# Value-pair operands in rows, and three small edits, in a one-layer hybrid decoder

## The chip, the cores and the metric

The kernel runs on one core of one Trainium2 chip, as one launch. The metric is the device time of an execution in microseconds; the time given for a kernel is the median of several runs. The profile of a kernel is one execution taken by the hardware profiler. Its engines are named PE (TensorE, matmuls), PEld (its weight loads), DVE (VectorE), ACT (ScalarE), POOL (GpSimd) and SP (SyncE, which issues the loads); L12 is line 12 of the kernel.

## The reference

One layer of a decoder on x of 512 tokens by 1024 channels, all in fp32:

```python
proj = x @ w_in                       # q, k, v of three mixers, and 3 x 1024 gate columns
o_da = diff_attention(...)            # 4 heads, two softmax maps each
o_sb = stick_breaking_attention(...)  # 8 heads of 64: A = sig(z) * prod of later (1 - sig(z))
o_dl = dilated_attention(...)         # 3 groups (dilation 1, 4, 16) x 4 heads of 128
merged = (g[:, :, 0] * (o_da @ w_branch_da) + g[:, :, 1] * (o_sb @ w_branch_sb)
          + g[:, :, 2] * (o_dl @ w_branch_dil))
x = layer_norm(ALPHA * x + merged @ w_out, ln1_g, ln1_b)
c = square(relu(x @ w_up)) @ w_down
ple = sigmoid(x @ w_ple_gate) * (p @ w_ple)        # p: 512 x 256, the embedding
x = layer_norm(ALPHA * x + c + ple, ln2_g, ln2_b)
```

## The kernel before, in words

Every fp32 operand of a large product is split into a high part rounded to the format fp32r and the rest, and a product is three matmuls: high by high, high by low, low by high. Weights stream from HBM in chunks of 128x1024 through a ring of six raw buffers (the loads are issued by SP); ScalarE casts a chunk to its high part `wh` (L243) and VectorE subtracts to get the low part `wl` (L245), each in a ring of six. x lies transposed in SBUF as `xhT` and `xlT`, eight blocks k of 128 channels by 512 tokens.

The work is a list of items, each a group of matmuls into a PSUM bank and an evacuation. A main loop goes through the items in order; before each item, and in the middle of those whose `mm` yields, it calls `step()`, which advances the attention heads that are active and the generators in `pending`. So heads' small matmuls are laid between the items of the projections. PSUM has two banks of the tag `mm` and six of the tag `at`; SBUF has 48 slots of 128x512 that all other tiles share. A tile gets a slot when its first write is scheduled, and that write waits until a slot is free. The order of each engine's instructions is laid out when the program is built, in program order as far as inputs and buffers allow, with ready instructions going ahead of blocked ones.

The last two groups of dilated values (`dl_v` 1 and 2) are computed together by `value_pair` as seven products of half-size blocks (p = 1, 2, 7, 6, 4, 5, 3 in that order, two items r = 0, 1 of 12 matmuls each, L465 to L467). The stationary operand of a matmul is here a piece of x, 128 channels by 128 tokens, where the tokens are those of one residue modulo 4. For p = 7, 6, 4 and 5 these pieces come from sums of x, made by `value_forms` from tiles `xr` (x loaded again, eight slots) into tiles `fr` and split into `u7`, `u6`, `u4` and `u5` with tokens side by side. For p = 1, 2 and 3 they are read in place, every fourth element of `xhT` and `xlT` (the table `vf`, L364). `value_forms` is put in `pending` four items ahead of the pair, waits `WAIT` = 5 steps, and then makes one form or its split a step.

Dilated head 0 runs at the same time: scores L1805 (dilation 1) and L1821 (the two others), biases and row maxima on VectorE (L1808, L1829), exponentials on ScalarE (L1814, L1836), small products L1846 and L1848 that bring the denominators of the groups together from `r0` (L1839) and `r1` (L1842), and later transposes L1889 and L1898.

A stick-breaking head (`sb_head`) holds its scores in three banks: key block 0 in 512 columns, block 1 in 384, and blocks 2 and 3 side by side in 256 each. After the logarithms, a product with a triangular matrix sums over later keys inside a block (L1666, high and low part), and products with ones (L1670) bring in the blocks behind.

`wout_items` multiplies the merged branches by `w_out`: two halves of 512 columns, four token tiles tt each, 24 matmuls over k = 0 to 7 (L887 to L889). Its stationary operands come from `merged_T[h, th, kp]`, transposes (L794) that ScalarE copies (L798) and VectorE subtracts from (L799): h is the half of k, th the half of the tokens. Those of th = 1 are turned between the first tiles: h = 1 after tile 0, h = 0 after tile 1. Then `ple_items` computes the embedding's product, eight items of six matmuls (L955 to L957) into `at` banks, evacuated by ScalarE (L961), while the first layer norm runs (L848 on ScalarE, L846 to L862 on VectorE) and its transposes (L924) lie between the items.

Of the kernel before, what the change touches and what calls it, by code (L numbers as in the profile page):

```python
# [10 lines left out]
F32 = mybir.dt.float32  # L11
F32R = mybir.dt.float32r  # L12
# [6 lines left out]
P = 128  # L19
# [36 lines left out]
def trunk(tc, a, out):  # L56
    nc = tc.nc
    es = ExitStack()
    with es:
# [14 lines left out]
        def slot(name, dt=F32):  # L74
            return big.tile([P, 512], dt, name=nm(name), tag="s", bufs=NSLOT)
# [190 lines left out]
        def item(cs, mm, ev, need=None, bank=None, size=1.0):  # L266
            items.append({"c": cs, "mm": mm, "ev": ev, "need": need, "bank": bank, "size": size})
# [7 lines left out]
        xhT = one.tile([P, 8, 512], F32R, name="xhT", tag="XH", bufs=1)  # L275
        xlT = one.tile([P, 8, 512], F32R, name="xlT", tag="XL", bufs=1)
        xh = [xhT[:, k, :] for k in range(8)]
        xl = [xlT[:, k, :] for k in range(8)]
# [49 lines left out]
        def first_item():  # L328
# [28 lines left out]
            def ev(ps):  # L357
# [3 lines left out]
        HB = slice(0, 256)  # L361
        HC = slice(256, 512)

        vf = {p: [[(xh[k][:, 2 * th + r::4], xl[k][:, 2 * th + r::4]) for r in range(2)] for k in range(ks, ks + 4)]  # L364
              for p, ks, th in ((1, 0, 0), (2, 4, 0), (3, 4, 1))}
        vsum = [[dram.tile([P, 1024], F32, name=f"vsum{m}_{i}") for i in range(2)] for m in range(2)]
        v_from = [None]

# [19 lines left out]
        def value_forms():  # L388

            xr = [slot("xr") for _ in range(8)]  # L390
            for k, t in enumerate(xr):
                i = nc.gpsimd.dma_start(t, xt[:, k, :])
                tc.add_manual_dep(getattr(i, "ins", i), lows[-1].name, mybir.DependencyInfo(
                    mybir.DependencyClass.Sync, mybir.DependencyReason.DATA), reason="not ahead of time")

            def blk(kh, k, th):
                return xr[4 * kh + k].rearrange("p (t c) -> p c t", c=4)[:, 2 * th:2 * th + 2, :]

            def new():
                ts = [slot("fr") for _ in range(2)]  # L400
                return ts, [ts[k // 2].rearrange("p (k c t) -> p k c t", k=2, c=2)[:, k % 2] for k in range(4)]

            def parts(p, ts):
                form(vf, p, ts)
                vf[p] = [[(h[:, r * P:r * P + P], lo[:, r * P:r * P + P]) for r in range(2)] for h, lo in vf[p]]

            def neg_sub(o, i, j):
                nc.vector.scalar_tensor_tensor(o, i, -1.0, j, op0=OP.mult, op1=OP.subtract)

            for _ in range(WAIT):  # L410
                yield
            f7, o7 = new()
            with tc.issue_after(st["low"]):
                for k in range(4):
                    nc.vector.tensor_sub(o7[k], blk(1, k, 1), blk(0, k, 1))
            parts(7, f7)
            yield
            f6, o6 = new()
            with tc.issue_after(st["low"]):
                for k in range(4):  # L420
                    neg_sub(o6[k], o7[k], blk(0, k, 0))
            yield
            parts(6, f6)
            yield
            f4, o4 = new()
            for k in range(4):
                neg_sub(o4[k], o6[k], blk(1, k, 0))
            yield
            parts(4, f4)
            yield  # L430
            yield
            f1, o1 = new()
            for k in range(4):
                nc.vector.tensor_sub(o1[k], blk(0, k, 0), blk(0, k, 1))
            yield
            parts(5, f1)
            yield

        WAIT = 5

# [436 lines left out]
        def wout_items():  # L877
            for half in range(2):
                cs = [chunk(a["wo"][half, c].rearrange("p k n -> p (k n)"), 1024) for c in range(4)]
                for tt in range(4):  # L880
                    def mm(ps, tt=tt, cs=cs):
                        for k in range(8):
                            c = cs[k // 2]
                            s = slice((k % 2) * 512, (k % 2) * 512 + 512)
                            h, lo = merged_T[k // 4, tt // 2, k % 4 // 2]
                            q = slice(k % 2 * 256 + tt % 2 * P, k % 2 * 256 + tt % 2 * P + P)
                            nc.tensor.matmul(ps, h[:, q], c["h"][:, s], start=k == 0, stop=False)  # L887
                            nc.tensor.matmul(ps, h[:, q], c["l"][:, s], start=False, stop=False)
                            nc.tensor.matmul(ps, lo[:, q], c["h"][:, s], start=False, stop=k == 7)  # L889

                    def ev(ps, tt=tt, half=half):
                        y = xn.pop((tt, half))
                        if not half:
                            x1sum[tt] = small("lsm", 2)
                        i = nc.vector.scalar_tensor_tensor(y, y, ALPHA, ps, op0=OP.mult, op1=OP.add,
                                                           accum_out=x1sum[tt][:, half:half + 1])
                        st["added"] = getattr(i, "ins", i)
                        x1[tt, half] = y
                        if half:
                            pending.append(ln1_gen(tt))  # L900
                    item(cs if tt == 3 else [], mm, ev, need=cs, bank=at_bank)
                    for t in {0: [(1, 1, 0), (1, 1, 1)], 1: [(0, 1, 0), (0, 1, 1)]}.get(tt, ()) if not half else ():
                        turn_item(*t)
# [41 lines left out]
        def ple_items():  # L945
            cs = [chunk(a["wp"][half].rearrange("p k n -> p (k n)"), 1024) for half in range(2)]
            for half in range(2):
                for tt in range(4):
                    def mm(ps, tt=tt, half=half):
                        c = cs[half]  # L950
                        for k in range(2):
                            s = slice(k * 512, k * 512 + 512)
                            q = slice(tt * P, tt * P + P)
                            h, lo = pTs[k]
                            nc.tensor.matmul(ps, h[:, q], c["h"][:, s], start=k == 0, stop=False)  # L955
                            nc.tensor.matmul(ps, h[:, q], c["l"][:, s], start=False, stop=False)
                            nc.tensor.matmul(ps, lo[:, q], c["h"][:, s], start=False, stop=k == 1)  # L957

                    def ev(ps, tt=tt, half=half):
                        t = slot("ple")  # L960
                        nc.scalar.copy(t, ps)  # L961
                        ple[tt, half] = t
                    item([cs[half]] if tt == 3 else [], mm, ev, need=cs, bank=at_bank)


        sums_first = set()
# [490 lines left out]
        tri_r = one.tile([P, P], F32R, name="tri_r")  # L1457
# [151 lines left out]
        def sb_head(hd):  # L1609
# [5 lines left out]
            bank = [at_bank() for _ in range(3)]  # L1615
            for kb, bi, c0, n in reversed(blk):
                m = mask_b.rearrange("p a b -> p (a b)") if kb == 3 else mask_b[:, 1, :]
                nc.tensor.matmul(bank[bi][:, c0:c0 + (n if kb == 3 else P)], identb, m, start=kb != 2, stop=False,
                                 skip_group_check=True)
# [3 lines left out]
            w = [512, 384, 512]  # L1623
            sph, spl, later = {}, {}, {}
            for bi in (2, 1, 0):
                n = w[bi]
                ps = bank[bi][:, :n]
# [9 lines left out]
                h = slot("sph", F32R)[:, :n]  # L1637
                lo = slot("spl", F32R)[:, :n]
# [7 lines left out]
                if bi == 2:  # L1646
# [3 lines left out]
                    hl = slot("smp", F32R)  # L1650
# [3 lines left out]
                elif bi == 1:  # L1654
                    nc.vector.tensor_add(e[:, 128:384], e[:, 128:384], sm)
                    h = slot("smh", F32R)[:, :n]
# [4 lines left out]
                yield  # L1661
            ah, al = {}, {}
            for kb, bi, c0, n in reversed(blk):
                ps = bank[bi][:, c0:c0 + n]
                for hl in (sph, spl):
                    nc.tensor.matmul(ps, tri_r, hl[bi][:, c0:c0 + n], start=False, stop=False, skip_group_check=True)  # L1666
                if kb < 3:
                    n2, hl = later[kb]
                    for t in hl:
                        nc.tensor.matmul(bank[bi][:, c0 + n - n2:c0 + n], ones_r, t, start=False, stop=False,  # L1670
                                         skip_group_check=True)
                if kb == 3:
                    continue
                n = w[bi]
                e = slot("a")[:, :n]
                nc.scalar.activation(e, bank[bi][:, :n], AF.Exp)
                h = slot("ah", F32R)[:, :n]
                lo = slot("al", F32R)[:, :n]
                nc.vector.tensor_copy(h, e)
                nc.vector.tensor_sub(lo, e, h.bitcast(F32))  # L1680
                ah[bi], al[bi] = h, lo
                if kb != 1:
                    yield
# [12 lines left out]
            t = slot("ot")  # L1696
# [461 lines left out]
```

## Time and profile before

| | |
|---|---|
| time, median of 3 runs | 1040.13 us (1039.84 to 1040.6) |
| the profiled execution | 1040.08 us |
| its span, first to last instruction | 1038.1 us |
| granted TensorE clock, mean | 0.998 |
| busy: PE, PEld | 1028.0, 881.2 us |
| busy: DVE, ACT, POOL | 787.0, 591.7, 180.1 us |
| moved by DMA | 249.21 MB |

The busy time of PE is a union of overlapping, modelled spans, so that it covers short waits too; how fast TensorE goes is read from the distance between the starts of its matmuls. The stages are found by time: the stick-breaking heads up to 226 us, the value pair from 235 to 278 us, w_out from 607 to 658 us, the embedding from 658 to 672 us. The timeline's columns are start and duration in us, engine, line, operation, tiles, shapes and count; a bracket gives the idle time of the engine before the instruction and who ended it.

### The profile page before, as it was taken

To read this page: it belongs to the slowest core of one execution; us is meant where nothing else is said; L and a number is where in the kernel's file an instruction comes from. 1 tells how busy PE (TensorE), PEld (TensorE's weight loads), DVE (VectorE), ACT (ScalarE), POOL (GpSimd) and SP (SyncE) were. 2 spreads that over 40 slices of the span, in tenths; PEclk is the share of its full clock that TensorE was granted. 3 is DMA by queue.
4 is the path that set the end of the run, shared out by engine and by line. 5 is a ranking of instruction groups with operands and counts; after the bars stand their busy time and mean duration, and the time that the engine had idled before them with its cause. 6 is when DMAs were issued, how large, how long until landed. Compare 5 with 4: busy or idle time off the path is not lost.

```text
span 1038.1 us, 15050 instructions
## 1 busy us (share of the span) xinstructions
PE 1028.0 (99%) x5448; PEld 881.2 (85%) x5448; DVE 787.0 (76%) x1412; ACT 591.7 (57%) x1010; POOL 180.1 (17%) x271
## 2 busy tenths in 40 slices
PE   9999999999999999999999999999999999999997
PEld 6888888889888888888888888889999889889886
DVE  6888667769765657779688885798768877877965
ACT  7566544536434645676675743775666556555651
POOL 0002411120211232411011040111111111111001
PEclk9999999999999999999999999999999999999999
DMA  8449968485976999977789795579999999998612
GB/s 309 121 156 271 277 193 217 120 290 144 285 182 222 271 272 294 238 205 199 227 269 235 267 320 182 160 222 319 331 290 315 301 306 340 303 295 279 235 57 81
DMA packets 71322, 249.21 MB, mean 240 GB/s; under 512 B 8808, under 2 KB 9592, under 8 KB 71248
## 3 DMA queue, kind: packets, MB, share of 16 engines
q0 software_dynamic: 32464, 116.21, 44.8%
q1 hardware_dynamic: 38208, 131.13, 35.1%
q8 instruction: 43, 0.70, 0.3%
q10 hardware_dynamic: 576, 0.92, 0.2%
q14 instruction: 31, 0.25, 0.1%
HBM read 246.10 MB, written 98.59 MB: 332 GB/s over the span
## 4 chain that ended last, share of the span: by engine, by line
PE 94%; DVE 2%; ACT 1%; DMA 1%; issue 1%; SPq 0%; POOL 0%; DVEq 0%; ACTq 0%; POOLq 0%
PE mm L87 10%; PE mm L88 10%; PE mm L89 10%; PE at L1261 4%; PE at L1262 4%; PE at L1263 4%; PE at L599 3%; PE at L600 3%; PE at L601 3%; PE mm L496 2%; PE mm L498 2%; PE mm L497 2%; PE at L89 1%; PE at L88 1%; PE at L87 1%; PE at L761 1%
## 5 line engine op out<-in xcount | busy, mean ns | idle before, releaser
L243 ACT CAST wh<-raw 128x1024 fp32r<-128x1024 f32 x257 | 268.6, 1049 | 242.0 <-PE mm L88 134.2
L245 DVE TENSOR_TENSOR wl<-raw,wh 128x1024 fp32r<-128x1024 f32 x257 | 312.7, 1223 | 112.9 <-ACT wh L243 111.3
L87 PE MATMUL mm<-xhT,wh 128*128 128x512 f32 x302 | 119.1, 394 | 0.0
L89 PE MATMUL mm<-xhT,wl 128*128 128x512 f32 x302 | 118.2, 391 | 0.0
L88 PE MATMUL mm<-xlT,wh 128*128 128x512 f32 x302 | 118.1, 391 | 0.0
L1261 PE MATMUL at<-wh,hh 128*128 128x512 f32 x188 | 73.7, 392 | 0.0
L87 PE MATMUL mm<-x1hT,wh 128*128 128x256 f32 x256 | 73.7, 288 | 0.0
L1262 PE MATMUL at<-wl,hh 128*128 128x512 f32 x188 | 73.7, 392 | 0.0
L1263 PE MATMUL at<-wh,hl 128*128 128x512 f32 x188 | 73.1, 389 | 0.0
L88 PE MATMUL mm<-x1lT,wh 128*128 128x256 f32 x256 | 72.2, 283 | 0.0
L89 PE MATMUL mm<-x1hT,wl 128*128 128x256 f32 x256 | 71.8, 283 | 0.0
L89 PEld LDWEIGHTS mm<-xhT,wl 128*128 128x128 f32 x302 | 56.8, 188 | 11.9
L87 PEld LDWEIGHTS mm<-xhT,wh 128*128 128x128 f32 x302 | 56.7, 188 | 11.0
L88 PEld LDWEIGHTS mm<-xlT,wh 128*128 128x128 f32 x302 | 56.7, 188 | 10.8
L87 PEld LDWEIGHTS mm<-x1hT,wh 128*128 128x128 f32 x256 | 48.7, 190 | 4.8 <-ACT up L1195 3.0
L88 PEld LDWEIGHTS mm<-x1lT,wh 128*128 128x128 f32 x256 | 48.8, 191 | 1.5
L89 PEld LDWEIGHTS mm<-x1hT,wl 128*128 128x128 f32 x256 | 48.6, 191 | 0.0
L1095 POOL DMA_DIRECT2D usum<-in_wu_dram x32 | 28.3, 921 | 101.6 <-DMA usum<-usum 34.8
L1095 POOL DMA_DIRECT2D dsum<-in_wd_dram x28 | 25.6, 936 | 102.5 <-DMA dsum<-dsum 37.0
L1263 PEld LDWEIGHTS at<-wh,hl 128*128 128x128 f32 x188 | 35.3, 188 | 7.7
L1261 PEld LDWEIGHTS at<-wh,hh 128*128 128x128 f32 x188 | 35.5, 189 | 6.0
L1262 PEld LDWEIGHTS at<-wl,hh 128*128 128x128 f32 x188 | 35.5, 189 | 5.5
(601 smaller groups left out, 2677.2 us busy)
## 6 DMA issues: line engine op xcount, KB each, us to landing
usum<-in_wu_dram POOLq DMA_DIRECT2D x48, 512.0 KB, 9.0
dsum<-in_wd_dram POOLq DMA_DIRECT2D x42, 512.0 KB, 8.9
raw<-in_wt_dram SPq DMA_DIRECT2D x38, 512.0 KB, 5.1
raw<-usum SPq DMA_DIRECT2D x32, 512.0 KB, 7.7
raw<-dsum SPq DMA_DIRECT2D x28, 512.0 KB, 7.0
raw<-in_wd_dram SPq DMA_DIRECT2D x25, 512.0 KB, 6.1
raw<-in_wu_dram SPq DMA_DIRECT2D x24, 512.0 KB, 7.6
raw<-in_wv_dram SPq DMA_DIRECT2D x18, 512.0 KB, 5.7
```

What stands on the lines that cost most here:

```text
L87: nc.tensor.matmul(ps, wh, xh, start=start, stop=False, skip_group_check=True)
L88: nc.tensor.matmul(ps, wh, xl, start=False, stop=False, skip_group_check=True)
L89: nc.tensor.matmul(ps, wl, xh, start=False, stop=stop, skip_group_check=True)
L243: i = nc.scalar.copy(h, raw)
L245: i = nc.vector.tensor_sub(lo, raw, h.bitcast(F32))
L599: nc.tensor.matmul(ps, h[:, q], c["h"][:, n], start=go, stop=False, skip_group_check=True)
L600: nc.tensor.matmul(ps, h[:, q], c["l"][:, n], start=False, stop=False, skip_group_check=True)
L601: nc.tensor.matmul(ps, lo[:, q], c["h"][:, n], start=False, stop=end, skip_group_check=True)
L1095: i = nc.gpsimd.dma_start(o, i, accum_op=OP.add, max_dma_last_dim=4096)
L1261: nc.tensor.matmul(ps, h[:, q], c["h"][:, s], start=go, stop=False, skip_group_check=True)
L1262: nc.tensor.matmul(ps, h[:, q], c["l"][:, s], start=False, stop=False, skip_group_check=True)
L1263: nc.tensor.matmul(ps, lo[:, q], c["h"][:, s], start=False, stop=end, skip_group_check=True)
```

## The change

Four edits. `in_rows` copies the strided pieces of x for p = 1, 2 and 3 by ScalarE into tiles `vh` and `vl` where a piece's 128 tokens lie side by side: eight copies of 128x256 into four slots for each p, in two steps of four. Those of p = 1 are made in the last two of the five steps that `value_forms` waits; those of p = 2 begin in the step that splits form 6, so that forms 4 and its split come one step later; those of p = 3 begin in the step that splits form 5. In the third tile of the first half of w_out the order of k is 4 to 7, then 0 to 3. The embedding's items of odd tt in the first half take a bank of the tag `mm`. In a stick-breaking head the triangular products of key blocks 2 and 3 become one of 512 columns for each of the two parts.

```diff
--- before.py
+++ after.py
@@ -361,8 +361,24 @@
         HB = slice(0, 256)
         HC = slice(256, 512)
 
-        vf = {p: [[(xh[k][:, 2 * th + r::4], xl[k][:, 2 * th + r::4]) for r in range(2)] for k in range(ks, ks + 4)]
-              for p, ks, th in ((1, 0, 0), (2, 4, 0), (3, 4, 1))}
+        vf = {}
+
+        def in_rows(p, ks, th):
+
+            vf[p] = []
+            for kp in range(2):
+                ts = []
+                for x, name in ((xhT, "vh"), (xlT, "vl")):
+                    t = slot(name, F32R)
+                    i = x[:, ks + 2 * kp:ks + 2 * kp + 2, :].rearrange("p k (t c) -> p k c t", c=4)
+                    o = t.rearrange("p (k c t) -> p k c t", k=2, c=2)
+                    for k in range(2):
+                        nc.scalar.copy(o[:, k], i[:, k, 2 * th:2 * th + 2].bitcast(F32))
+                    ts.append(t)
+                vf[p] += [[tuple(t[:, 256 * k + r * P:256 * k + r * P + P] for t in ts) for r in range(2)]
+                          for k in range(2)]
+                yield
+
         vsum = [[dram.tile([P, 1024], F32, name=f"vsum{m}_{i}") for i in range(2)] for m in range(2)]
         v_from = [None]
 
@@ -407,8 +423,9 @@
             def neg_sub(o, i, j):
                 nc.vector.scalar_tensor_tensor(o, i, -1.0, j, op0=OP.mult, op1=OP.subtract)
 
-            for _ in range(WAIT):
+            for _ in range(WAIT - 2):
                 yield
+            yield from in_rows(1, 0, 0)
             f7, o7 = new()
             with tc.issue_after(st["low"]):
                 for k in range(4):
@@ -421,20 +438,19 @@
                     neg_sub(o6[k], o7[k], blk(0, k, 0))
             yield
             parts(6, f6)
-            yield
+            yield from in_rows(2, 4, 0)
             f4, o4 = new()
             for k in range(4):
                 neg_sub(o4[k], o6[k], blk(1, k, 0))
             yield
             parts(4, f4)
             yield
-            yield
             f1, o1 = new()
             for k in range(4):
                 nc.vector.tensor_sub(o1[k], blk(0, k, 0), blk(0, k, 1))
             yield
             parts(5, f1)
-            yield
+            yield from in_rows(3, 4, 1)
 
         WAIT = 5
 
@@ -878,15 +894,17 @@
             for half in range(2):
                 cs = [chunk(a["wo"][half, c].rearrange("p k n -> p (k n)"), 1024) for c in range(4)]
                 for tt in range(4):
-                    def mm(ps, tt=tt, cs=cs):
-                        for k in range(8):
+                    ks = (4, 5, 6, 7, 0, 1, 2, 3) if tt == 2 and not half else range(8)
+
+                    def mm(ps, tt=tt, cs=cs, ks=ks):
+                        for k in ks:
                             c = cs[k // 2]
                             s = slice((k % 2) * 512, (k % 2) * 512 + 512)
                             h, lo = merged_T[k // 4, tt // 2, k % 4 // 2]
                             q = slice(k % 2 * 256 + tt % 2 * P, k % 2 * 256 + tt % 2 * P + P)
-                            nc.tensor.matmul(ps, h[:, q], c["h"][:, s], start=k == 0, stop=False)
+                            nc.tensor.matmul(ps, h[:, q], c["h"][:, s], start=k == ks[0], stop=False)
                             nc.tensor.matmul(ps, h[:, q], c["l"][:, s], start=False, stop=False)
-                            nc.tensor.matmul(ps, lo[:, q], c["h"][:, s], start=False, stop=k == 7)
+                            nc.tensor.matmul(ps, lo[:, q], c["h"][:, s], start=False, stop=k == ks[-1])
 
                     def ev(ps, tt=tt, half=half):
                         y = xn.pop((tt, half))
@@ -960,7 +978,8 @@
                         t = slot("ple")
                         nc.scalar.copy(t, ps)
                         ple[tt, half] = t
-                    item([cs[half]] if tt == 3 else [], mm, ev, need=cs, bank=at_bank)
+                    item([cs[half]] if tt == 3 else [], mm, ev, need=cs,
+                         bank=None if tt % 2 and not half else at_bank)
 
 
         sums_first = set()
@@ -1661,9 +1680,9 @@
                 yield
             ah, al = {}, {}
             for kb, bi, c0, n in reversed(blk):
-                ps = bank[bi][:, c0:c0 + n]
-                for hl in (sph, spl):
-                    nc.tensor.matmul(ps, tri_r, hl[bi][:, c0:c0 + n], start=False, stop=False, skip_group_check=True)
+                for hl in (sph, spl) if kb != 2 else ():
+                    nc.tensor.matmul(bank[bi][:, :w[bi]], tri_r, hl[bi], start=False, stop=False,
+                                     skip_group_check=True)
                 if kb < 3:
                     n2, hl = later[kb]
                     for t in hl:
```

## The prediction

> **What bounds the kernel now.** I read the page first: span, busy shares and the chain that ended last.
>
> ```profile
> span 1038.1 us, 15050 instructions
> ...
> PE 1028.0 (99%) x5448; PEld 881.2 (85%) x5448; DVE 787.0 (76%) x1412; ACT 591.7 (57%) x1010; POOL 180.1 (17%) x271
> ...
> PE 94%; DVE 2%; ACT 1%; DMA 1%; issue 1%; SPq 0%; POOL 0%; DVEq 0%; ACTq 0%; POOLq 0%
> ```
>
> TensorE is busy for 99% of the span and carries 94% of the chain. A change therefore pays only where it shortens TensorE's own stream or closes a hole in it, and it costs wherever TensorE comes to wait. The profiled execution took 1040.08 us: 1038.1 of span and 1.98 around it. It lies 0.05 below the median of the runs, 1040.13, so one sum serves for both. A measurement of this kernel can tell about 0.2% from no change, that is 2.08 us: faster means below 1038.05 and slower above 1042.21.
>
> Then I read the weight loads of the value pair by line (columns: shortest, median and longest ns, first and last start) and the timeline of TensorE and its loads (start us, duration us).
>
> ```profile
> L465 PEld LDWEIGHTS at<-wh,xhT x16: 308/310/311, 239.7 to 277.6; 128*128 128x128 f32 x16
> ...
> L465 PEld LDWEIGHTS mm<-wh,u6h x4: 188/188/188, 254.6 to 256.7; 128*128 128x128 f32 x4
> ...
> 272.67 0.31 PEld L465 LDWEIGHTS at<-wh,xhT 128*128 128x128 f32 x1
> ...
> 278.31 1.71 PEld L1910 LDWEIGHTS at<-pt,dl_v 128*128 128x128 f32 x8
> ...
> 254.65 0.19 PEld L465 LDWEIGHTS mm<-wh,u6h 128*128 128x128 f32 x1
> ...
> 260.08 0.19 PEld L465 LDWEIGHTS mm<-wh,u4h 128*128 128x128 f32 x1
> ...
> 239.71 0.60 PE L465 MATMUL at<-wh,xhT 128*128 128x512 f32 x1
> 240.15 0.40 PE L466 MATMUL at<-wl,xhT 128*128 128x512 f32 x1
> ...
> 263.71 0.47 PE L465 MATMUL at<-wh,u4h 128*128 128x512 f32 x1
> 264.03 0.39 PE L466 MATMUL at<-wl,u4h 128*128 128x512 f32 x1
> ...
> 243.45 0.30 PEld L1846 LDWEIGHTS at<-r,fold 128*128 128x128 f32 x2 [0.40 <-DVE r L1839]
> ```
>
> A load with every fourth element of x takes 310 ns, one from a row 188.
>
> **Rows for products 1, 2 and 3.** Product 3 is 24 matmuls between 272.67 and 278.31: 5.64 us. Product 6, from rows, takes 260.08 - 254.65 = 5.43 us. The difference is 0.21, and three products have strided operands: 0.63 us less. The load thus stays mostly hidden, as it is prefetched under the matmul before it. It shows where the matmuls before are short: after the small matmuls of dilated head 0 the second strided matmul starts 0.44 us after the first (239.71 to 240.15), in rows 0.32 (263.71 to 264.03). Such blocks (L1805, L1821, L1846, L1848) stand four times ahead of a strided matmul: 4 x 0.12 = 0.48 us less.
>
> The Trainium skill, TensorE: Matmul & The Clock Gate, LDWEIGHTS (loading the stationary operand), makes the load a matter of its column count alone; by it rows would gain nothing here. The trace disagrees, 310 against 188 ns with the same 128 columns. The skill's SBUF - State Buffer, on the 16-byte lines under Door 1: The DMA port swizzle, charges each access that crosses into a new line, which four fp32 elements of step do; the two durations agree with that one, and it would charge the new copies as well.
>
> What the rows add is 24 ScalarE copies of 128x256.
>
> ```profile
> L1195 ACT COPY up<-mm 128x256 f32<-128x256 f32 x16 | 5.8, 363 | 0.0
> ...
> L271 ACT CAST u6h<-fr x2: 620/621/622, 232.1 to 233.2; 128x512 fp32r<-128x512 f32 x2
> ...
> L408 DVE SCALAR_TENSOR_TENSOR fr<-fr,xr x8: 610/620/640, 230.9 to 240.7; 128x256 f32<-128x256 f32 x8
> ...
> L1201 DVE TENSOR_TENSOR hid<-mm,up x16: 417/425/425, 714.8 to 957.7; 128x256 f32<-128x256 f32 x16
> ...
> 220.00:225.00 5.00, 5.00 (x25) 4.06 (x24) 3.67 (x6) 1.06 (x1) 0.99 (x2) 1.00 1.05 374
> 225.00:230.00 5.00, 5.00 (x25) 4.20 (x24) 3.33 (x6) 2.89 (x5) 0.00 (x0) 1.00 0.86 278
> 230.00:235.00 5.00, 5.00 (x26) 4.22 (x24) 4.86 (x8) 2.57 (x4) 0.52 (x1) 1.00 0.55 206
> 235.00:240.00 5.00, 5.00 (x31) 4.96 (x30) 3.61 (x13) 2.16 (x9) 0.00 (x0) 1.00 0.32 113
> ```
>
> No row shows ScalarE reading SBUF at this step. From below it costs the contiguous copy of the same size, 0.36 us; from above a contiguous one of twice the size, 0.62. VectorE pays 620 instead of 425 ns for 256 elements where it reads x at this step, 0.2 more, so I take 0.5, between them: 12 us for 24, 4 for each product (2.9 to 5.0). ScalarE (the fourth busy figure of the windows) does 1.06 + 2.89 + 2.57 + 2.16 = 8.7 us in 220 to 240, so 11.3 are free. The eight copies of product 1, due at 235, and the eight of product 2, due at about 242, need 8 (5.8 to 9.9). They fit, and cost TensorE nothing, if they get their buffers in time. Without that cover product 2 starts late by what is left of its 4 us. Those of product 3 are made at the items of product 7, ahead of product 6 and so 18 us (254.65 to 272.67) before their use.
>
> Buffers are the tight point.
>
> ```profile
> 239.10 2.24 DVE L408 SCALAR_TENSOR_TENSOR fr<-fr,xr 128x256 f32<-128x256 f32 x4 [1.35 <-PE at L1821]
> ...
> 237.84 0.40 ACT L1814 ACTIVATE L<-L,nm 128x128 f32<-128x128 f32 x1 [3.06 <-DVE nm L1812]
> ...
> 239.78 0.59 ACT L472 COPY dl_v<-mm 128x512 f32<-128x512 f32 x1
> ...
> 243.21 0.18 DVE L1839 TENSOR_TENSOR r<-st,exf 128x32 f32<-128x32 f32 x1
> ...
> 214.51 1.05 ACT L243 CAST wh<-raw 128x1024 fp32r<-128x1024 f32 x1 [5.11 <-PE mm L88]
> ```
>
> L408 reads nothing that L1821 writes; it waits because its new tile takes a slot that L1821's operands hold. Counting the code's live tiles at 238 us I get all 48 slots: 4 outputs of heads, 4 bias tables, 4 value tiles, 16 q and k tiles, 8 of xr, 2 fr, 8 of u7 and u6, 2 of L0. The change wants up to 8 more there. Two things give way without harm: u6, cast by 234 and first read at 254.65, and form 4 (L408), which the change puts one step later. The copies wait for nothing but a slot, so the build may also set them earlier: ScalarE idles 5.11 us ahead of 214.51, and the same count of tiles leaves 8 slots free at 213. I take no stall from slots in the forecast and keep it as a rival.
>
> The later form 4 also moves 2.24 us of VectorE work from ahead of L1829 and L1839, for which TensorE's L1846 idles 0.40. With the copies near L1814, whose sums L1839 reads, I count half of it, 0.20 (from 0.40 gained to some microseconds lost, below).
>
> **Third w_out tile.** It now begins with k 4 to 7, whose transposes were turned after the first tile, and reads those just turned 2.7 us (12 matmuls of 0.226) later.
>
> ```profile
> 623.19 1.03 PE L794 MATMUL mm<-ident,b 128*128 128x128 f32 x8
> ...
> 624.47 0.50 PE L887 MATMUL at<-wh,mh 128*128 128x512 f32 x1 [0.24 <-ACT mh L798]
> ...
> 659.55 1.03 PE L924 MATMUL at<-ident,xn 128*128 128x128 f32 x8
> ...
> 660.34 0.48 PE L955 MATMUL at<-wh,pTh 128*128 128x512 f32 x1
> ```
>
> Eight transposes to the next matmul take 1.28 us here and 0.79 where nothing is waited for: 0.49 less. Next would be the second turned pair, whose ScalarE copy stands right behind the first one's: covered.
>
> **Embedding on both pools.** Two of its tiles move to the two banks of the other pool, idle at that point.
>
> ```profile
> 664.29 0.39 PE L957 MATMUL at<-wh,pTl 128*128 128x512 f32 x1
> 664.90 0.50 PE L955 MATMUL at<-wh,pTh 128*128 128x512 f32 x1 [0.21 <-ACT ple L961]
> ...
> 663.56 0.72 ACT L848 ACTIVATE junk<-xn,lnm 128x512 f32<-128x512 f32 x1 [1.76 <-DVE lnm L846]
> ...
> 664.28 0.56 ACT L961 COPY ple<-at 128x512 f32<-128x512 f32 x1
> ```
>
> The fifth tile finds six banks taken until ScalarE, itself held by the layer norm, empties the first: 0.61 us between matmuls instead of 0.23, 0.38 less. Next late would be the layer norm's transposes between the tiles (L924), none of which waits now; I count no loss (up to the whole 0.38 if they come to wait as long).
>
> **Triangular products.** Four of 256 columns become two of 512, eight heads.
>
> ```profile
> 114.28 0.28 PE L1666 MATMUL at<-sph,tri_r 128*128 128x256 f32 x1
> ...
> 114.75 0.28 PE L1670 MATMUL at<-sph,ones_r 128*128 128x256 f32 x1
> ...
> 122.68 0.40 PE L1666 MATMUL at<-sph,tri_r 128*128 128x512 f32 x1
> ...
> 123.15 0.34 PE L1670 MATMUL at<-smh,ones_r 128*128 128x384 f32 x1
> ```
>
> Four narrow ones take 0.47 us (114.28 to 114.75), two wide ones 0.47 (122.68 to 123.15): nothing. Both halves of the bank are split at once before, so no new wait arises.
>
> **Sum.** 0.63 + 0.48 + 0.20 + 0.49 + 0.38 = 2.18; 1040.08 - 2.18 = 1037.9. With the whole 0.40 it is 1037.7; a further 0.7, two stalls of the size seen that dissolve as the order shifts, gives 1037.0.
>
> **Rivals.** *Rows late for product 2 (slower).* If the build does not put the copies early, the second product's rows find slots only as the first product's are released, its last matmul at about 239.71 + 2.8 = 242.5. Eight copies then hold ScalarE until 246.5, and if head 0's exponentials (from 237.84 to 239.78 now, 2 us) stand behind them, L1839 comes at 248.5 and L1846, fixed in TensorE's order inside product 2, runs at 248.7 instead of about 243.1: 5.6 lost, 1037.9 + 5.6 = 1043.5. It becomes slower than the threshold once the loss passes 4.3 us. For it speaks the count of 48 of 48 and the wait of L408; against it the idle ScalarE before 220 and 8 us of tiles that can be put off.
>
> *Rows partly late (no change).* Slots come at 239 to 240, from L1821's operands, so the first half of product 2 is in time and the second late by 1 to 2 us: 1039 to 1040.
>
> *Rows that do not speed TensorE (the edit does not do what it says).* If the spacing of the strided products is not the loads' doing, the 0.63 and 0.48 stay: 1037.9 + 1.1 = 1039.0. Against it speaks that only these products are spaced so. The skill's rule of column counts would give this time.
>
> **How the numbers follow.** Forecast 0.50, its own range 1037.0 to 1038.05. Partly late 0.15 and rows without effect 0.07, both within 0.2%. Late for product 2: 0.28, high because three unknowns (price of the copies, place in the queue, slots) all point to it, and because a new order can shift other waits. So faster 0.50, same 0.22, slower 0.28. The range runs from 1037.0, the bottom of the forecast, to 1043.5, past the no-change cases to the price of the slower one, leaving about 0.15 above and 0.05 below.
>
> **What would show it.** Right: loads of 188 ns in all of L465 to L467, 5.43 us for product 3, no idle time at L1846, 0.8 us from L794 to L887, 0.23 before the fifth embedding tile, copies of 0.4 to 0.6 us done before 242. Wrong: idle TensorE at the start or middle of product 2 released by a ScalarE copy or a VectorE r, xr loads or the last stick-breaking head waiting for slots before 225, or new waits in the layer norm after 664.

## The result, and the profile after

The changed kernel takes 1045.13 us (median of 6 runs, 1043.27 to 1045.64), the kernel before 1039.99 beside it (6 runs, 1039.60 to 1041.02). The ratio is 1.0044, with a 95% interval of 1.0031 to 1.0057: slower by about 5 us, where 1037.9 was forecast. Two executions far outside the others of their kernel, 1283.77 us with 16 unread copies and 3647.12 us with rows for products 1 and 3, count in the numbers of runs below but not in the ratios.

The page of the changed kernel, its span and busy times (in its line numbers; the value pair's matmuls are now L481 to L483, the copies L376):

```profile
span 1043.3 us, 15051 instructions
...
PE 1030.1 (99%) x5432; PEld 877.7 (84%) x5432; DVE 787.3 (75%) x1412; ACT 604.7 (58%) x1034; POOL 180.0 (17%) x271
```

TensorE is still busy 99% of the span. The 24 copies are ScalarE's 13.0 us more (604.7 against 591.7), 0.54 each. The value pair's weight loads by line (shortest, median and longest ns), and from TensorE's timeline the places of w_out and the embedding:

```profile
L481 PEld LDWEIGHTS at<-wh,vh x16: 187/188/331, 239.9 to 284.6; 128*128 128x128 f32 x16
```

```profile
629.14 1.03 PE L810 MATMUL mm<-ident,b 128*128 128x128 f32 x8
629.93 0.48 PE L905 MATMUL at<-wh,mh 128*128 128x512 f32 x1
...
669.70 0.39 PE L975 MATMUL mm<-wh,pTl 128*128 128x512 f32 x1
669.93 0.39 PE L973 MATMUL at<-wh,pTh 128*128 128x512 f32 x1
```

Loads from rows take 188 ns, as forecast. From the eight transposes (L810) to w_out's next matmul it is 0.79 us instead of 1.28, and the embedding's fifth tile follows the matmul before it after 0.23 instead of 0.61: both as forecast. What is new is among TensorE's waits (us in total, times, longest):

```profile
PE at L1865 <- DVE r L1858: 2.4, 1, 2.4
...
PE at L1908 <- DVE L L1889: 0.5, 1, 0.5
PE at L1867 <- DVE r L1861: 0.5, 1, 0.5
PE mm L481 <- DVE dl_v L493: 0.4, 1, 0.4
```

L1865 is L1846 of before, the product that needs head 0's `r0`. In the timeline of TensorE, and then in windows of 2 us (the figure after POOL's is the granted clock):

```profile
245.35 0.40 PE L483 MATMUL mm<-wh,vl 128*128 128x512 f32 x1
248.15 0.41 PE L1865 MATMUL at<-r,fold 128*128 128x32 f32 x2 [2.40 <-DVE r L1858]
248.39 0.59 PE L481 MATMUL at<-wh,vh 128*128 128x512 f32 x1
248.78 0.63 PE L482 MATMUL at<-wl,vh 128*128 128x512 f32 x1
...
251.77 0.51 PE L483 MATMUL at<-wh,vl 128*128 128x512 f32 x1
252.12 0.39 PE L481 MATMUL at<-wh,vh 128*128 128x512 f32 x1
```

```profile
248.00:250.00 2.00, 1.85 (x6) 1.53 (x7) 0.09 (x1) 0.00 (x0) 0.42 (x1) 0.65 0.85 119
250.00:252.00 2.00, 2.00 (x6) 1.55 (x5) 0.84 (x7) 1.22 (x2) 0.00 (x0) 0.50 1.01 188
```

After 2.40 us without work the clock stands at 0.50, and eight matmuls go by 0.43 us apart instead of 0.23. The busy share shows none of that: but for the end of the hole, those windows are full.

To see where the time went, I set the same weight products of TensorE side by side in two traces and subtracted their starts (the columns are the places in the kernel before; each row is a kernel minus the kernel before, us):

```
place in before           45 us   230    246.0  246.3  248.1   289    615    629    665    678    end
after                     -0.15  +0.30  -0.66  +2.14  +3.64  +5.81  +5.94  +5.41  +5.04  +5.19  +5.22
no rows                   -0.57  -0.12  -0.12  -0.12  -0.12  -0.11  -0.10  -0.63  -1.01  -0.88  -0.86
tiles without time        -0.25  +0.22  -0.50  +0.75  +0.95  +3.05  +3.05  +2.51  +2.14  +2.28  +2.31
hole filled               -0.50  -0.04  -1.01  +1.78  +1.84  +3.89  +3.95  +3.41  +3.04  +3.18  +3.22
w_out and embedding only  +0.04  +0.03  +0.03  +0.03  +0.03  +0.04  +0.09  -0.44  -0.81  -0.67  -0.61
u6 late, all rows         -0.29  +0.16  -0.32  -0.32  -0.36  +0.92  +1.58  +1.04  +0.67  +0.81  +0.83
rows 1, 3, no merge       -0.64  -0.64  -1.27  -1.26  -1.26  -1.57  -1.46  -2.00  -2.37  -2.21  -2.18
```

The first row: 0.45 lost up to 230 us. Product 1 then gains 0.27 (+0.03 at 242.5), and the 0.69 more that seem won by 246.0 are the `r0` product with its wait, which stood at 243.4 before and now stands in the hole: 2.80 there, 2.11 net. The slow clock costs 1.50, later waits and shifts to the end of the pair 2.17; then 0.53 gained at w_out (615 to 629), 0.37 at the embedding (629 to 665) with 0.15 given back in the layer norm. The first column, and differences of a few tenths that begin there, are the start of the kernel, of which nothing is explained here. The lower rows are experiments below.

Why is `r0` late? VectorE's and ScalarE's timelines of the changed kernel:

```profile
237.61 0.68 DVE L272 TENSOR_TENSOR u6l<-fr,u6h 128x512 fp32r<-128x512 f32 x1
239.38 0.69 DVE L272 TENSOR_TENSOR u6l<-fr,u6h 128x512 fp32r<-128x512 f32 x1 [1.09 <-issue]
240.22 0.69 DVE L324 COPY dl_k<-mm 128x512 f32<-128x512 f32 x1
241.36 0.29 DVE L1827 CUSTOM_DVE_ANT_0 L<-at,shf 128x128 f32<-128x128 f32 x1 [0.46 <-PE at L482]
...
243.82 0.16 DVE L1831 TENSOR_SCALAR nm<-st 128x4 f32<-128x4 f32 x1
...
247.90 0.19 DVE L1858 TENSOR_TENSOR r<-st,exf 128x32 f32<-128x32 f32 x1 [0.65 <-ACT L L1833]
...
239.32 1.23 ACT L376 CAST vh<-xhT 128x256 fp32r<-128x256 f32 x2 [2.37 <-PE at L1840]
...
243.86 1.19 ACT L376 CAST vl<-xlT 128x256 fp32r<-128x256 f32 x2
244.96 1.04 ACT L243 CAST wh<-raw 128x1024 fp32r<-128x1024 f32 x1
245.90 0.40 ACT L1833 ACTIVATE L<-L,nm 128x128 f32<-128x128 f32 x1
```

Product 2's copies start at 239.32, released by L1840, the score products whose q and k tiles then come free. The second low half of u6 goes at 239.38, the same moment, after a gap that the trace puts down to issue, that is to nothing it shows. Behind it on VectorE stand the key copy (240.22, before 234.49) and head 0's scores (241.36, before 236.22). `nm`, 237.58 before, comes at 243.82, and the exponential that needs it starts 1.9 us after its end, at 245.90, behind copies and weight casts on ScalarE. 48 tiles hold everything, so two things are mixed here: tiles and ScalarE's time.

### The profile page after: what moved, and what is told of

Its sections match the earlier page's. It is cut to its first block, busy times and chain, and to the rows that moved or that the text cites. A ratio compares the mean times of both kernels' runs of the same rounds, so it can differ in the third digit from the quotient of the medians.

```text
span 1043.3 us, 15051 instructions
## 1 busy us (share of the span) xinstructions
PE 1030.1 (99%) x5432; PEld 877.7 (84%) x5432; DVE 787.3 (75%) x1412; ACT 604.7 (58%) x1034; POOL 180.0 (17%) x271
## 4 chain that ended last, share of the span: by engine, by line
PE 96%; DVE 2%; ACT 1%; DMA 0%; issue 0%; DVEq 0%; ACTq 0%
PE mm L87 10%; PE mm L89 10%; PE mm L88 10%; PE at L1280 4%; PE at L1281 4%; PE at L1282 4%; PE at L615 3%; PE at L616 3%; PE at L617 3%; PE mm L512 2%; PE mm L514 2%; PE mm L513 2%; PE at L89 1%; PE at L87 1%; PE at L88 1%; PE at L907 1%
## 5 line engine op out<-in xcount | busy, mean ns | idle before, releaser
L87 PEld LDWEIGHTS mm<-xhT,wh 128*128 128x128 f32 x302 | 56.7, 188 | 11.3 <-PE mm L514 0.2
```

Of the source, the lines that this page charges most:

```text
L87: nc.tensor.matmul(ps, wh, xh, start=start, stop=False, skip_group_check=True)
```

## The experiments

The theory: product 1's and 2's rows take tiles that u6 and the scores need, instructions that wait for a tile hold what is queued behind them, `r0` comes 4.7 us later and TensorE pays that with a hole and a low clock. The rival: ScalarE's 13 us are too much where they stand.

**No rows.** The changed kernel with `vf` and `value_forms` of before.

> The changed kernel without its rows: the value pair reads x strided as before, w_out, embedding and triangular edits stay. Theory (all of the loss is made in the value pair by the rows): w_out and embedding give 0.53 and 0.4 us, so about 1039.2 us (1038.6 to 1039.8), with no idle time of more than 0.5 us ahead of the matmuls that read r in head 0 and the granted clock at 1.00 from 240 to 260 us. Rival (one of the three other edits shifts the schedule and makes a good part of the loss): above 1041 us.

1039.87 us (11 runs), 0.07 above the expected range, against 1040.39 for the kernel before beside it, ratio 0.9996 (0.9987 to 1.0005), no wait at head 0, clock 1.00. The loss lies in the rows. Its time cannot be told from before; its row above shows two real gains and one loss, taken up below.

**Forms first.** All rows; form 4 right behind form 6, u6's and u4's casts later and, by `issue_after`, behind the newest weight chunk's low part (the edit, shortened).

```diff
-            parts(6, f6)
-            yield from in_rows(2, 4, 0)
             f4, o4 = new()
             ...
+            yield from in_rows(2, 4, 0)
+            with tc.issue_after(st["low"]):
+                parts(6, f6)
             yield
-            parts(4, f4)
+            with tc.issue_after(st["low"]):
+                parts(4, f4)
```

> The changed kernel with all its rows and all 24 copies, but with form 4 made right after form 6 (which gives back four xr tiles early) and the casts of u6 and u4 put off until product 2's rows are asked for: fewer tiles are live between 234 and 255 us. Theory (tiles are short, and the copies stand ahead of head 0's exponentials in ScalarE's queue for that reason): scores and exponentials are back near 236 and 239 us, r0 near 243.5 instead of 247.90, the 2.4 us wait of the fold matmul falls under 0.6, the clock stays at 1.00, and about 1037.8 us comes out (1037.2 to 1039). Rival (ScalarE's time for the copies is what is lacking, whatever the tiles): r0 still 3 us late, 1042.5 to 1045.

1046.37 us (5 runs), ratio 1.0055 (1.0043 to 1.0068): a miss for the theory's time. Yet `r0` came at 243.73, as it said; it is `r1` (L1863) that is late, and TensorE asked for `r0` sooner. TensorE's waits, and VectorE's timeline:

```profile
PE at L1869 <- DVE r L1863: 2.4, 1, 2.4
PE at L1867 <- DVE r L1860: 1.4, 1, 1.4
```

```profile
247.88 0.69 DVE L272 TENSOR_TENSOR u6l<-fr,u6h 128x512 fp32r<-128x512 f32 x1 [2.02 <-ACT u6h L271]
248.49 0.17 DVE L1854 TENSOR_SCALAR nm<-st 128x4 f32<-128x4 f32 x1
```

The casts of u6 were put where head 0's second `nm` stands right behind them on VectorE, and they wait for ScalarE, which has copies ahead of them. The stall was moved, not removed.

**Copies without tiles.** Two kernels from the one before, with unread copies into one spare tile, asked for at the places of the real ones, the operands still strided: 24 copies, then only the 16 of products 1 and 2 (the edit, shortened).

```diff
+            junk = slot("vj", F32R)
+            def dummy(ks, th): ...   # nc.scalar.copy into junk, two to a tile, eight to a product
             for _ in range(WAIT - 2):
                 yield
+            yield from dummy(0, 0)   # and dummy(4, 0); in the first kernel dummy(4, 1) too
```

> The kernel before, with 24 ScalarE copies of the same sizes and at the same places in the program, all into one spare tile that nobody reads; the products read x strided as before. ScalarE pays the whole 13 us, but only one tile more is live. Rival (ScalarE's time in front of the exponentials makes the loss): r0 3 to 5 us late, 1043 to 1045 us. Theory (the shortage of tiles makes it): r0 under 1 us late, since the copies are done when ScalarE would idle, 1040.0 to 1041.0 us.

> The kernel before with 16 unread ScalarE copies into one spare tile, those of products 1 and 2 only (with 24 such copies all of them stood between 219 and 238 us, product 3's too, and left ScalarE no gap). ScalarE pays 9 us between 219 and 236 us, no tiles are taken. Theory (in the changed kernel tiles are short): the copies fit into ScalarE's gaps, scores back at 236 to 237 us, r0 under 0.5 us late, 1040.0 to 1041.0 us. Rival (9 us of ScalarE are too much by themselves, because the weight casts and the casts of u7 and u6 queue behind them): r0 2 us late or more, 1042.5 to 1045 us.

With 24: 1044.88 us (5 runs), ratio 1.0041 (1.0027 to 1.0054), inside the rival's range. But with no tile to wait for, all 24 went into 219 to 238 us, product 3's too, and ScalarE had no gap (5.00 us busy in 220 to 225, 4.97 and 4.98 in the next two windows); a weight cast came at 237.74 instead of 233.75, and the scores behind it. With the 16 that the changed kernel has ahead of this point:

```profile
235.92 0.68 DVE L324 COPY dl_k<-mm 128x512 f32<-128x512 f32 x1
...
237.66 0.28 DVE L1823 CUSTOM_DVE_ANT_0 L<-at,shf 128x128 f32<-128x128 f32 x1
...
243.21 0.18 DVE L1854 TENSOR_TENSOR r<-st,exf 128x32 f32<-128x32 f32 x1
```

1039.92 us (11 runs), ratio 0.9999 (0.9991 to 1.0008), just under the theory's range. Scores 1.4 us late, `r0` at 243.21, to the hundredth where it was before. With no tile to wait for, all 16 were done by 232.4 us. So the time of 16 copies is covered where nothing holds them back, and that of 24 is not; the changed kernel made the second eight of them only from 239.32 on.

**Tiles without time.** The changed kernel, with only the last-read block of each row tile of products 1 and 2 copied (the edit, shortened; product 3 keeps its copies).

```diff
-                    for k in range(2):
-                        nc.scalar.copy(o[:, k], i[:, k, 2 * th:2 * th + 2].bitcast(F32))
+                    nc.scalar.copy(t[:, 384:512], i[:, 2 * th + 1].bitcast(F32))   # i: block k = 2 * kp + 1
```

> The changed kernel, but for products 1 and 2 each row tile holds only the block that is read last (one copy of 128x128 for a tile instead of two of 128x256); the other three quarters of the operands are read strided. The tiles are taken and held as long as in the changed kernel, ScalarE pays a quarter or so. Theory (tiles are short): the scores of head 0 still wait for tiles until 240 us, 1042 to 1044.5 us. Rival (ScalarE's time makes the loss): r0 back near 243.5 us, 1039.3 to 1040.5 us.

```profile
239.38 0.69 DVE L272 TENSOR_TENSOR u6l<-fr,u6h 128x512 fp32r<-128x512 f32 x1 [2.44 <-issue]
240.21 0.69 DVE L324 COPY dl_k<-mm 128x512 f32<-128x512 f32 x1
241.51 0.29 DVE L1836 CUSTOM_DVE_ANT_0 L<-at,shf 128x128 f32<-128x128 f32 x1 [0.60 <-PE at L491]
...
246.52 0.19 DVE L1867 TENSOR_TENSOR r<-st,exf 128x32 f32<-128x32 f32 x1 [0.65 <-ACT L L1842]
```

1042.61 us (8 runs), ratio 1.0026 (1.0016 to 1.0036), inside the theory's range. With a third of ScalarE's time for these copies (product 2's take 1.70 us instead of 4.84), u6's second low half, key copy and scores stand within 0.15 us of where they stand in the changed kernel. So tiles set that delay, and the unnamed gap in front of u6's low half ends at 239.38 in both. The copies' length adds the last 1.4 us of `r0` (246.52 to 247.90). The hole is 0.84 us here, and the clock stays at 1.00. What is lost behind it, from 248.1 to 289 us, is 2.10, about the 2.17 of the changed kernel, with the same three waits of 0.5, 0.5 and 0.4: this part comes with the tiles and the new order, and not with the copies' time or the clock.

**The hole filled.** 14 unread matmuls ahead of L1865, released by head 0's first exponential, which the edit, shortened, calls `e0`.

```diff
             px = at_bank()
+            if hd == 0:
+                for _ in range(14):
+                    i = nc.tensor.matmul(px[:, 256:512], xh[0][:, 0:P], xh[0][:, 0:256], ...)
+                    tc.add_manual_dep(i.ins, e0.name, ...)
```

> The changed kernel with 14 unread matmuls of 256 columns, released by head 0's first exponential, directly ahead of the fold matmul that waits for r0: they fill some 1.5 us of the 2.8 us in which TensorE idles and are over when r0 comes. Theory (the idle time itself takes the clock to 0.5 for about 3.4 us, which costs 1.7 us beyond the idle time): clock 1.00 from 246 to 256 us, and 1043.2 to 1043.8 us where the changed kernel has 1045.1. Rival (the clock falls for another reason): 1045 to 1046 us, the clock as low as without them.

```profile
246.09 1.94 PE L1869 MATMUL at<-xhT 128*128 128x256 f32 x14 [0.68 <-ACT L L1833]
247.87 0.34 PE L1873 MATMUL at<-r,fold 128*128 128x32 f32 x2
248.04 0.48 PE L481 MATMUL at<-wh,vh 128*128 128x512 f32 x1
```

```profile
248.00:250.00 2.00, 2.00 (x12) 1.66 (x11) 0.29 (x3) 0.47 (x1) 0.07 (x1) 1.00 0.91 137
250.00:252.00 2.00, 2.00 (x10) 1.67 (x9) 1.90 (x16) 1.98 (x3) 0.00 (x0) 1.00 0.94 186
```

1043.41 us (5 runs), as the theory said and 1.7 less than the changed kernel. In the table the stretch from 246.0 to 246.3 costs 2.79 as there (2.80), but the next, to 248.1, 0.06 instead of 1.50: the products are as late, only TensorE was kept busy, and the clock stayed at 1.00. Two of the changed kernel's own six runs, 1043.27 and 1043.92, have a mean clock of 0.999 and 0.998 where the others have 0.997, which fits a drop that they missed in whole or part.

**Rows for product 3 alone; rows for 1 and 3 with u6 late.** In the first kernel `in_rows` of products 1 and 2 becomes plain steps and u6 stays where it is; the edit of the second, shortened:

```diff
-            parts(6, f6)
-            yield from in_rows(2, 4, 0)
+            yield
             f4, o4 = new()
             for k in range(4):
                 neg_sub(o4[k], o6[k], blk(1, k, 0))
+            parts(6, f6)
```

> The changed kernel with rows for product 3 alone (8 copies, made at 266 to 270 us, when tiles are free again), products 1 and 2 strided. Theory (rows save time where their tiles are there, the loss belongs to the rows of product 2): 0.2 to 0.45 us below the version without rows, 1038.8 to 1039.2 us, no wait ahead of the fold matmuls. Rival (copies on ScalarE cost wherever they stand): 0.5 us or more above the version without rows.

> The changed kernel with rows for products 1 and 3 (16 copies), product 2 strided, form 4 at its step of before, and the casts of u6 behind form 4, so that product 1's four tiles take the place of u6's four. Theory (rows gain where tiles are to be had): no wait for tiles between 230 and 245 us, r0 at 243.2 us as before, 0.2 us from product 1 and 0.2 from product 3 below the version without rows: 1039.2 to 1039.6 us. Rival (any copy ahead of head 0 delays it): 1041 us or more.

1039.68 us (11 runs; 1.0001, 0.9991 to 1.0012) and 1039.39 (12 runs; 0.9995, 0.9986 to 1.0003). Neither can be told from before by time; the first is 0.5 above its expected range (and two of its runs, 1043.46 and 1044.76, lie 4 to 5 us above its median, unexplained), the second inside. Side by side with the kernel before, product 3's rows gain 0.18 in the first (+0.46 at 248 us to +0.28 at 289), and in the second the pair gains 0.93 (+0.37 at 230 to -0.56).

**u6's casts moved.** All rows, and u6's casts behind form 4. Besides, product 2's copies and form 4 come one step earlier than in the changed kernel, form 4 to its step of before, so that this run can't tell the three apart.

```diff
-            yield
-            parts(6, f6)
             yield from in_rows(2, 4, 0)
             f4, o4 = new()
             for k in range(4):
                 neg_sub(o4[k], o6[k], blk(1, k, 0))
+            parts(6, f6)
             yield
             parts(4, f4)
             yield
+            yield
```

> The changed kernel with one thing moved: the casts of u6 (four tiles) come behind form 4 instead of behind form 6, and form 4 is back at its step of before. All rows and all 24 copies stay. Theory (the low halves of u6 wait for a tile at the head of VectorE's queue until 239.38 us, with the key copy and head 0's scores behind them): without them product 2's copies get u6's tiles by 236 us, scores come at 237 us, r0 at 243 to 244 us, no TensorE wait over 0.5 us in the value pair, 1038.2 to 1039.2 us. Rival (with all rows some other tile wait takes its place): copies or scores wait until 239 us again, 1041 us or more.

```profile
PE mm L481 <- ACT dl_v L488: 0.7, 1, 0.7
...
PE at L1867 <- DVE r L1861: 0.2, 1, 0.2
```

```profile
239.19 0.69 DVE L324 COPY dl_k<-mm 128x512 f32<-128x512 f32 x1 [1.04 <-PE at L1840]
...
244.66 0.19 DVE L1858 TENSOR_TENSOR r<-st,exf 128x32 f32<-128x32 f32 x1
```

1040.68 us (11 runs), ratio 1.0005 (0.9996 to 1.0014): 4.4 us less than the changed kernel, most of its loss, and the hole is gone. The key copy still waits for a tile, until 239.19 against 240.22, so the theory named a step that counts but not the only tile that is short: it expected 1038.2 to 1039.2, and scores at 237, where they come at 240.08. The pair loses 0.76 where rows for two products gain 0.93; ScalarE makes product 3's copies ahead of an evacuation (the 0.7 above).

**Without the merge.** The w_out and embedding edits alone; then the two versions above without merged triangular products.

```diff
-                for hl in (sph, spl) if kb != 2 else ():
-                    nc.tensor.matmul(bank[bi][:, :w[bi]], tri_r, hl[bi], ...)
+                for hl in (sph, spl):
+                    nc.tensor.matmul(ps, tri_r, hl[bi][:, c0:c0 + n], ...)
```

> The kernel before with the w_out and embedding edits alone: neither rows nor merged triangular products. In the traces so far every version with merged triangular products stands 0.45 us later at 230 us than its own start, every version without them 0. Theory (the merge costs about 0.45 us in the stick-breaking stage, since it moves two narrow products in TensorE's order): 0.3 to 0.5 us below the version with the three edits, 1039.2 to 1039.5 us, and no drift between 45 and 230 us. Rival (the merge is worth nothing, as predicted): 1039.6 to 1039.9 us.

> The version before this one (u6 late, all rows) without the merged triangular products. Theory: a further 0.3 to 0.5 us less, 1037.8 to 1038.8 us, the fastest of all. Rival (merge worth nothing): the same as the version before this one.

> Rows for products 1 and 3, u6 late, w_out and embedding edits, without the merged triangular products. Theory: 0.3 to 0.5 us below the same with the merge (1039.39 us), so 1038.8 to 1039.1 us; 0.4 to 0.8 us above the version with rows for product 2 too, whose loads save 0.2 us and its entries behind the dilated blocks another 0.2 to 0.5. Rival (rows of product 2 cost what they gain): the same as with them.

1039.29 us (11 runs; 0.9991, 0.9982 to 1.0000), 1040.42 (11 runs; 1.0001, 0.9992 to 1.0010) and 1038.01 (10 runs; 0.9977, 0.9968 to 0.9986), beside 1040.25 for the kernel before. The first is in its expected range, the second 1.6 above, the third 0.8 below. The last is the fastest kernel of the study, 2.2 us below the kernel before, and its interval lies clear of 1. In its trace 1.54 of the 2.18 us come after 45 us (-0.64 to -2.18); the rest lies in the start, which isn't explained. In the side-by-side traces the drift from 45 to 230 us is +0.45 with the merge (also +0.45 and +0.46 in the versions above) and 0.00, -0.01 and -0.02 in these three. Rows for product 2 too were expected to gain 0.4 to 0.8 us; that version is 2.4 us slower (1040.42 against 1038.01).

Where part of it arises, in TensorE's timeline and its loads in the changed kernel:

```profile
61.70 0.39 PE L88 MATMUL mm<-xlT,wh 128*128 128x512 f32 x1
62.07 0.38 PE L1708 MATMUL at<-ah,sb_v 128*128 128x256 f32 x1
...
62.06 0.19 PEld L1708 LDWEIGHTS at<-ah,sb_v 128*128 128x128 f32 x1 [0.40 <-DVE sb_v L525]
```

Fewer triangular instructions pull a value product of the head before one matmul ahead, where its operand is not ready: 0.24 us. The rest comes by some 0.04 at each of the five heads after 94 us and wasn't traced.

## Why the prediction was wrong

What happened is the first rival, rows late for product 2, with a chance of 0.28 and a price of 1043.5, and 1.6 us beyond it. The step that failed is one sentence: "I take no stall from slots in the forecast". It put a term at nothing for which the prediction itself had the count of 48 of 48 tiles and the wait of L408. In its place the runs showed `r0` 4.7 us late, 3.3 of it also with a third of the copies' time, and from that 2.11 us of hole, 1.50 of low clock and 2.17 of later waits and shifts.

- **Rows, 0.63 + 0.48.** Right in kind and about right in size. The loads are 188 ns. Product 3's rows gave 0.18 to 0.19 (forecast 0.21); product 1 gave 0.27 in the changed kernel from 230 to 242.5 us, its entry behind L1840 0.32 instead of 0.44. A stream of strided loads costs TensorE a little, as said.
- **L1846, 0.20.** Wrong in the changed kernel, where a hole of 2.40 came. And the 0.40 was misread: it is the idle time of the weight loads (PEld). TensorE's own matmuls are 0.48 apart there (242.97 to 243.45) where 0.23 is usual, so 0.25 was to be had, and not 0.40. With rows for 1 and 3 alone the product waits for nothing and its place gives 0.35, but by another route than the forecast's: form 4 is back at its step there, and u6 comes later (`r0` stands at 241.16 in the version without the merge).
- **Copies at 0.5 us, 11.3 us free.** Each cost 0.54. The cover was there for 16 of them (1039.92 with 16 unread copies) and not for 24. The Trainium skill, ScalarE: Activation LUTs, What ACT_TABLE_LOAD costs, also gives the time of an activation without pointer operands, 186 ns and 0.833 for each element, less 93 back to back; by it, an estimate, 256 elements cost 0.31 us. The measured 0.54 is well above; the copies read every fourth element, which that rule does not count.
- **Form 4 a step later "also moves 2.24 us of VectorE work" away, and u6 and form 4 "give way without harm".** Wrong, and this is the mechanism as far as the traces show it. u6 did not give way: its second low half went on VectorE only at 239.38, when tiles came free, ahead of what head 0 needs, and the key copy and the scores came behind it. That it waited for a tile is inferred, since the trace names no releaser; with the casts moved the key copy itself waited until 239.19. Form 4 came at 253.75 instead of 239.10, and kept four `xr` tiles that long.
- **The rival's route** was copies in ScalarE's queue ahead of L1814. That was the smaller half: about 1.4 us of `r0`'s 4.7. Its price of 5.6 is near the 5.8 lost from 242.5 to 289 us (+0.03 to +5.81), but the sum is another: 2.1 of hole, 1.5 of low clock, 2.2 of later waits and shifts. So its number came near by luck, and the clock was not in the prediction at all.
- **w_out 0.49, embedding 0.38.** 0.53 and 0.37, with 0.15 of the latter given back in the layer norm, where "no loss" was counted and up to the whole 0.38 bounded.
- **Triangular products 0.** The products themselves cost the same, as worked out, but "no new wait arises" was wrong: the order around them cost 0.45.

The lines for L1846, from TensorE's timeline before:

```profile
242.97 0.40 PE L466 MATMUL mm<-wl,xhT 128*128 128x512 f32 x1
243.45 0.41 PE L1846 MATMUL at<-r,fold 128*128 128x32 f32 x2
```

What stays open: why the traces differ by up to 1.0 us in the first 45 us, 0.3 to 0.7 us that some versions lose between 289 and 615 us, what makes up the 2.1 us lost behind the hole beyond the waits named, and which of the moved steps wins back the most.

## What to carry to other kernels

When tiles are all taken, price an added tile by what stands behind the first instruction that will wait for one, on each engine's queue; free time on the engine that makes the tile says nothing about it. Test tiles and time apart: the same copies into one spare tile, and the same tiles with a third of the copying. And an edit that saves nothing by count can still cost through the order it gives the others: a merge worth 0 by count cost 0.45 us, where all the other edits together won 1.5 in the fastest version.

## What the runs showed of the hardware

A hole of 2.40 us took TensorE's clock to 0.50 for 3.4 us (248.6 to 252.0) and cost 1.5 to 1.7 us on top; one of 2.52 us in the version with 24 unread copies took it to 0.50 for 6.8 us. In the forms-first version a hole of the same 2.40 left the clock at 1.00 in the execution profiled:

```profile
251.67 0.41 PE L1869 MATMUL at<-r,foldT 128*128 128x32 f32 x2 [2.40 <-DVE r L1863]
```

The traces' records of the clock tell the two apart. In each of the traces the changes of the clock lie whole multiples of 3.413 us apart (in the changed kernel 71, 1 and 231 of them), so that they fall on a grid. Here are two steps of that grid in the changed kernel, and two in the forms-first version (columns as in the windows above; the second figure is TensorE's busy time):

```profile
245.19:248.60 3.41, 1.01 (x6) 0.57 (x5) 1.42 (x2) 2.68 (x9) 0.87 (x1) 1.00 0.85 143
248.60:252.02 3.42, 3.42 (x9) 2.65 (x9) 0.86 (x7) 1.24 (x2) 0.00 (x0) 0.50 0.91 144
```

```profile
247.62:251.03 3.41, 1.65 (x8) 1.03 (x6) 3.15 (x5) 3.41 (x10) 0.70 (x1) 1.00 0.00 0
251.03:254.44 3.41, 2.77 (x13) 2.37 (x14) 2.87 (x8) 3.41 (x7) 1.05 (x2) 1.00 0.77 115
```

In the changed kernel the whole hole lies in one step of the grid; TensorE is busy for 1.01 us of it, and the next step has the low clock. With 24 unread copies it is 1.22 (242.05 to 245.47). In the forms-first version the grid splits the hole into 1.76 and 0.64 us, TensorE is busy for 1.65 us in the step with the first part, and the clock stays at 1.00. So in these traces it counts where a hole lies, and not only how long it is. The other runs of the forms-first version, 1046.15 to 1047.17 us at a mean clock of 0.996 to 0.998, are up to 3.2 us longer, which fits a hole that fell otherwise; they have no trace.

The Trainium skill, TensorE: Matmul & The Clock Gate, Part 1, lets a free-running window of 3.4 us decide. The grid and the length of the low clock agree with that. By its table the clock falls "after ≥1 idle window"; here a window with 1.01 us of work in it was enough.
